# The four operand sums of an FFN chunk pair: made in the up stage from the tiles on chip and stored, instead of in the down stage

## The chip, the cores and the metric

The kernel runs on one core of one Trainium2 chip. The metric is the device time of one execution in microseconds (us); the median of three runs stands for the kernel. Engines: PE (TensorE matmul), DVE (VectorE), ACT (ScalarE), POOL (GpSimd), and SP (SyncE), which here only issues DMAs.

## The reference

One layer of a streaming encoder on 1024 tokens and 16 meta tokens, 1024 channels, in float32. The change lies in the last third, the convolutional FFN:

```python
def _conv_ffn(xn, w_up, conv_w, conv_b, w_down):
    hid = xn @ w_up                                   # 1024 -> 2 * 2816
    hp = jnp.pad(hid, ((0, 0), (CONV_WIDTH - 1, 0), (0, 0)))
    conv = conv_b + sum(hp[:, j:j + seq_len] * conv_w[j] for j in range(CONV_WIDTH))
    val, gate = jnp.split(conv, 2, axis=-1)
    return (jax.nn.silu(gate) * val) @ w_down         # 2816 -> 1024
```

Before it come an RMSNorm and a mixer (forgetting attention beside a state-space branch, merged and projected); behind it the residual sum, a final RMSNorm, and the meta tokens are dropped.

## The kernel before, in words

Every float32 matmul is made of three PE products of rounded parts: each operand is split into hi (a copy on ACT that rounds) and lo (operand minus hi, function `split_lo`, line 137, on DVE or POOL). One logical product so costs hi·hi, hi·lo and lo·hi.

**Up stage (about 790 to 1230 us of the span).** The 2816 hidden channels are worked off in 22 chunks of 128; chunk c needs a gate block and a value block of `w_up`. Chunks 0, 1, 2 and 21 are made plainly (`plain_pair`); chunks 3 to 20 by `block_pair`, in which `seven` (line 213) replaces the eight block products of a 2x2 blocked matmul by seven, with sums of the weight blocks (`weight_forms`, `combine`: tiles `sf`, POOL, line 1286), split by ACT (line 1160) and DVE (line 137) into a ring of 8 tiles `sw`, and with sums of the token blocks that are made once. The seven products are put together from PSUM (banks `mm`, `sp`, `tp`) with ACT copies and DVE adds (line 238) into `hg` and `hv` (128 x 1026, in a ring of three); `c1`, `u2` and `u3` are scratch of `seven`. `seven` is also called once in the mixer (the GLU). Then the convolution of width 3: one ACT instruction (line 1336) and two DVE instructions (line 1338) for each of `og` and `ov` (lines 1197 and 1199 in plain chunks). `glue` (line 1167) makes the chunk's result: silu on ACT (line 1168), the product of value and gate on POOL (line 1169), and a store of 512 KB by SP to `a_d` in DRAM (line 1170). `og` and `ov` have one buffer each. Raw weights (`raw`) are loaded by SP, three buffers. During the up stage, `down_weight_sums` also makes the sums of `w_down`'s blocks in DRAM (`t_d`) by accumulating DMAs on POOL's queue (line 1304) and copies on SP's.

**Down stage (about 1230 us to the end).** The product with `w_down` is also made by seven products over 2x2 blocks. Pair j holds chunks 2j and 2j+1; a11 and a21 are the left and right token halves (512 each) of chunk 2j, a12 and a22 those of chunk 2j+1. The 11 pairs are summed in four groups of pairs, [0-1], [2-4], [5-7], [8-10]; in each group the products run in the order 0, 4, 1, 2, 5, 3, 6. `load_pair` loads a pair's four halves (tiles `ar`, SP, line 1376) when the group's first product is prepared. `forms` (line 1380) prepares one product of one pair: it loads the weight (`wr`, SP, line 1383, a ring of 8), makes the operand's sum in place on POOL for products 1, 2, 3 and 6 (lines 1388, 1390, 1392, 1394), rounds operand and weight on ACT (line 1400), and splits off lo on POOL for products 0, 4 and 5, else on DVE. The results go to operand slots, 14 in all (`op`, and the former token tiles `xhi`, `xlo`). `product` (line 1437) issues the matmuls (lines 1455 to 1457: for a group of three pairs 36 of 512 columns, nine into each of four PSUM banks) and adds the PSUM banks into `u2`, `hs` on DVE (line 1465). `finish` makes the final norm.

The order of instructions on each engine is not that of the code: a scheduler, which simulates the program's times, decides it from the dependences. So a change of code can move instructions that it doesn't touch.

Of the kernel before, what the change touches and what calls it, by code (L numbers as in the profile page):

```python
# [9 lines left out]
F = mybir.dt.float32  # L10
# [4 lines left out]
ALU = mybir.AluOpType  # L15
# [43 lines left out]
def block_kernel(ctx, tc, x, meta, xbt, x0t, g1t, w_q, w_k, w_v, w_f, w_u, w_g, b_f, w_ao, lam_d, bw_d, cw_d,  # L59
# [56 lines left out]

    to_d = {p: dp.tile([D // 2, 512], F, name=f"to_d{p}") for p in (1, 2, 3, 5)}
    t_d = {p: dp.tile([DFF // 2, 512], F, name=f"t_d{p}") for p in (1, 2, 3, 5)}

    def stack(pl, t, n):  # L120
        s_ = pl.tile([P, KD, 64], R, tag="stk", name="stk")
# [91 lines left out]
    def seven(pl, A, B, kh, pieces, shift, top, bot):  # L213
# [4 lines left out]
        wide = max(n for _, n in pieces)  # L218
        st = []
        for p0, n in pieces:  # L220
            c1, u2, u3 = (pl.tile([P, wide], F, tag=tag, name=tag, bufs=2)[:, :n] for tag in ("c1", "u2", "u3"))
            st.append(dict(p0=p0, n=n, c1=c1, u2=u2, u3=u3, l=slice(p0, p0 + n),
                           r=slice(shift + p0, shift + p0 + n)))

        def prod(q, key, bank, a, b):
            joins = bank is None
# [15 lines left out]
        for q in st:  # L242
            add(q["u2"], prod(q, "b", s_ps, S2, T2), q["c1"])
        for q in st:
            S.copy(top[:, q["l"]], prod(q, "a", None, A12, B21))
        for q in st:
            add(q["u3"], prod(q, "b", None, S3, T3), q["c1"])
        for q in st:
# [918 lines left out]
    def glue(g_, v_, c):  # L1167
        S.activation(g_, g_, AF.Silu)  # L1168
        (V if c == NFF - 1 else GP).tensor_tensor(v_, v_, g_, ALU.mult)  # L1169
        (S if c == NFF - 1 else SY).dma_start(a_d[P * c:P * c + P], v_)  # L1170

    def conv_out(m, tag):
        if m % NFF == NFF - 1:

            return ha.tile([P, SEQ], F, tag="h", name=tag, bufs=3, padded_shape=[P, 2 * NH])
        return ha.tile([P, SEQ], F, tag=tag, name=tag)

    def plain_steps(c, parts=(QBLK,), ws={}):
        res = []
# [78 lines left out]
            SY.dma_start(h2[:, 4:], xc[:, 4:])  # L1258
    st_sm.close()
    ha = pool(st_r, "hid", side="right")  # L1260
    for tag in ("og", "ov"):
        ha.tile([P, SEQ], F, tag=tag, name=tag)
    normed(0, hm, 2)

    first_pair = plain_steps(0, ([(514, 256), (770, 254)], [(0, 258), (258, 256)]), early)
# [102 lines left out]
    def behind(ld, j):  # L1368
        if h_load and j in groups[1]:
            after(ld, h_load[-1])  # L1370

    def load_pair(j):
        for k in range(2):
            c0 = P * (2 * j + k)
            for h_ in range(2):
                behind(SY.dma_start(raw_tile(j, k, h_), a_d[c0:c0 + P, 512 * h_:512 * h_ + 512]), j)
# [1 line left out]
    n_op = [0]  # L1378

    def forms(p, j):  # L1380
        r = pairs[j]
        b_ = down1.tile([P, 512], F, tag="w", name="wr", bufs=8)
        behind(SY.dma_start(b_, w_block(*own_w[p], j) if p in own_w else t_d[p][P * j:P * j + P]), j)

        a11, a21, a12, a22 = (r[k, h_] for k in range(2) for h_ in range(2))
        sub, add = ALU.subtract, ALU.add
        if p == 1:
            GP.tensor_tensor(a11, a11, a21, sub)
        elif p == 2:
            GP.tensor_tensor(a11, a22, a11, add)  # L1390
        elif p == 3:
            GP.tensor_tensor(a21, a22, a21, sub)
        elif p == 6:
            GP.tensor_tensor(a11, a11, a12, sub)
        slot = ops[n_op[0] % len(ops)]
        n_op[0] += 1
        a_ = (a11, a11, a11, a21, a12, a22, a11)[p]
        eng = GP if p in (0, 4, 5) else V
        for q, src in ((0, a_), (2, b_)):
            hi = S.copy(slot[q], src)  # L1400
            if first_copy and j < 2 and p >= 5:
                after(hi, first_copy[1])
            cut = split_lo(eng, slot[q + 1], src, slot[q])
            if first_add and eng is V and j < 2 and p > 2:
                after(cut, first_add[1 if p == 3 else 3])
        return slot
# [88 lines left out]
    def prepare():  # L1495

        while len(ready) < (len(items) if first_add else 3) and room[0] >= len(groups[items[len(ready)][0]]):
            g, p = items[len(ready)]
            room[0] -= len(groups[g])
            if p == 0:  # L1500
                for j in groups[g]:
                    load_pair(j)
            ready[g, p] = [forms(p, j) for j in groups[g]]

    dpool[0] = down1
    for j in groups[0]:
        load_pair(j)
    for p in ORDER[:2]:
        room[0] -= 2
        ready[0, p] = [forms(p, j) for j in groups[0]]  # L1510
# [423 lines left out]
```

## Time and profile before

| | us |
|---|---|
| runs | 1465.48, 1460.87, 1460.35 |
| median | 1460.87 |
| profiled execution | 1462.22 |
| its span, first to last instruction | 1460.1 |
| mean granted PE clock | 0.994 |
| PE busy | 1429.3 |
| DVE / POOL / ACT busy | 1075.5 / 758.5 / 721.9 |

All details are from the one profiled execution. A row of the timeline gives the start in us, the duration, engine, source line, operation, output tile <- input tiles, shape, and in square brackets the idle time before it with the instruction that ended it. A row of the waits gives the waiting group, what ended its waits, their sum in us, their number, and the longest. A row of the groups gives line, engine, operation, tiles, shape and count, then busy time and mean ns of one, then idle time before and what ended it. A row of DMA issues gives tiles, queue, count, KB each and the median us from issue to landing. A row of stretches gives the busy time of each engine with its instructions, the granted PE clock (1 is full), the DMA engines' share and GB/s.

### The profile page before, as it was taken

What the parts mean: (1) busy time and instruction counts of PE and PEld (TensorE: products, weight loads), DVE (VectorE), ACT (ScalarE), POOL (GpSimd) and SP (SyncE); (2) the same over time, 40 slices, a digit from 0 to 9 for tenths busy, and PEclk for the clock granted to TensorE, in tenths of its full rate; (3) what the DMA queues carried; (4) which work ended last, traced back from release to release, by engine and by line L of the source; (5) the groups of instructions that cost most, each with busy time, mean ns of one, the idle gap of its engine ahead of it and who ended that gap; (6) DMA issues with size and microseconds to landing.
All of it is one profiled execution on the core that took longest, in us unless ns stands there. A gap on an engine that the chain in (4) does not pass through costs nothing. (4 is left out here: it accounts for less than half of the span.)

```text
span 1460.1 us, 26545 instructions
## 1 busy us (share of the span) xinstructions
PE 1429.3 (98%) x9646; PEld 1350.1 (92%) x9646; DVE 1075.5 (74%) x2200; ACT 721.9 (49%) x1421; POOL 758.5 (52%) x890
## 2 busy tenths in 40 slices
PE   8999999999999999999999999999999999998997
PEld 8999999988999999999889999999999999786886
DVE  7999788842757676656479977888887666788685
ACT  7646576422646565533646444444444435642433
POOL 1542147631556556425861235546544427889766
PEclk9999999999999999999999999999999999999998
DMA  7685644630137422167954246667753224866413
GB/s 288 171 188 161 150 111 115 161 116 30 37 124 164 128 65 69 41 234 249 251 149 145 73 109 177 177 174 176 172 138 109 87 83 150 302 196 179 132 36 115
DMA packets 89717, 209.31 MB, mean 143 GB/s; under 512 B 14498, under 2 KB 22322, under 8 KB 89204
## 3 DMA queue, kind: packets, MB, share of 16 engines
q1 hardware_dynamic: 70068, 162.55, 34.1%
q0 software_dynamic: 17792, 41.41, 14.8%
q10 hardware_dynamic: 1728, 3.68, 0.7%
q8 instruction: 76, 1.25, 0.4%
q14 instruction: 53, 0.43, 0.1%
HBM read 168.52 MB, written 69.35 MB: 163 GB/s over the span
## 5 line engine op out<-in xcount | busy, mean ns | idle before, releaser
L170 PE MATMUL mm<-xhi,whi 128*128 128x342 f32 (+2 forms) x480 | 156.9, 327 | 1.5 <-DVE q L137 1.0
L171 PE MATMUL mm<-xlo,whi 128*128 128x342 f32 (+2 forms) x480 | 155.6, 325 | 0.0
L172 PE MATMUL mm<-xhi,wlo 128*128 128x342 f32 (+2 forms) x480 | 155.4, 324 | 0.0
L1169 POOL TENSOR_TENSOR ov<-ov,og 128x1024 f32<-128x1024 f32 x21 | 51.1, 2434 | 124.5 <-ACT og L1168 120.6
L137 DVE TENSOR_TENSOR sw<-sf,sw 128x512 fp32r<-128x512 f32 x72 | 68.9, 957 | 51.7 <-ACT sw L1160 51.6
L1160 ACT CAST sw<-sf 128x512 fp32r<-128x512 f32 x72 | 44.9, 624 | 105.6 <-POOL sf L1286 71.7
L170 PEld LDWEIGHTS mm<-xhi,whi 128*128 128x128 f32 x480 | 90.6, 189 | 2.9 <-PE sp L804 0.8
L171 PEld LDWEIGHTS mm<-xlo,whi 128*128 128x128 f32 x480 | 90.6, 189 | 0.4 <-issue 0.2
L172 PEld LDWEIGHTS mm<-xhi,wlo 128*128 128x128 f32 x480 | 90.4, 189 | 0.3
L853 ACT CAST th<-tp 128x256 fp32r<-128x256 f32 (+3 forms) x120 | 56.1, 472 | 62.1 <-PE tp L846 29.4
L137 DVE TENSOR_TENSOR tl<-tp,th 128x256 fp32r<-128x256 f32 (+3 forms) x120 | 65.1, 547 | 25.1 <-ACT th L853 23.6
L1286 POOL TENSOR_TENSOR sf<-raw 128x512 f32<-128x512 f32 x36 | 47.5, 1319 | 68.4 <-ACT sw L1160 22.1
L1286 POOL TENSOR_TENSOR sf<-raw,sf 128x512 f32<-128x512 f32 x36 | 59.9, 1663 | 44.4 <-DVE sw L137 43.2
L234 PE MATMUL mm<-xhi,sw 128*128 128x258 f32 (+1 forms) x288 | 81.1, 282 | 0.0
L232 PE MATMUL mm<-xhi,sw 128*128 128x258 f32 (+1 forms) x288 | 80.9, 281 | 0.0
L233 PE MATMUL mm<-xlo,sw 128*128 128x258 f32 (+1 forms) x288 | 80.8, 281 | 0.0
L818 POOL TENSOR_SCALAR pt<-pt,nm 128x144 f32<-128x144 f32 (+4 forms) x72 | 52.2, 738 | 50.4 <-DVE nm L817 49.5
L1338 DVE SCALAR_TENSOR_TENSOR ov<-hv,cwt,ov 128x1024 f32<-128x1024 f32 x36 | 72.1, 2003 | 0.2
L1160 ACT CAST sw<-raw 128x512 fp32r<-128x512 f32 x70 | 43.0, 621 | 49.0 <-PE sp L234 22.3
L816 ACT ACTIVATE pt<-pt,nm 128x144 f32<-128x144 f32 (+4 forms) x72 | 52.9, 736 | 27.0 <-DVE nm L815 26.6
L809 DVE CUSTOM_DVE_ANT_0 pt<-sp,fb 128x328 f32<-128x328 f32 (+8 forms) x112 | 46.4, 430 | 19.5 <-PE sp L804 11.3
L137 DVE TENSOR_TENSOR sw<-raw,sw 128x512 fp32r<-128x512 f32 x70 | 55.0, 788 | 5.2 <-ACT sw L1160 4.7
(715 smaller groups left out, 5732.6 us busy)
## 6 DMA issues: line engine op xcount, KB each, us to landing
raw<-in_w_up_dram SPq DMA_DIRECT2D x44, 512.0 KB, 3.8
t_d<-in_w_dn_dram POOLq DMA_DIRECT2D x44, 256.0 KB, 6.7
ar<-a_d SPq DMA_DIRECT2D x44, 256.0 KB, 5.3
wr<-t_d SPq DMA_DIRECT2D x44, 256.0 KB, 2.8
a_d<-ov SPq DMA_DIRECT2D x21, 512.0 KB, 2.6
wr<-in_w_dn_dram SPq DMA_DIRECT2D x33, 256.0 KB, 4.2
t_d<-in_w_dn_dram SPq DMA_DIRECT2D x22, 256.0 KB, 4.2
t_d<-t_d SPq DMA_DIRECT2D x22, 256.0 KB, 4.7
```

The lines of the kernel that those rows point to most:

```text
L137: return eng.tensor_tensor(out_, src, hi.bitcast(F), ALU.subtract)
L170: yield PE.matmul(ps, whi[:, i, :], ahi[:, i], start=(i == 0), stop=False)
L171: yield PE.matmul(ps, whi[:, i, :], alo[:, i], start=False, stop=False)
L172: yield PE.matmul(ps, wlo[:, i, :], ahi[:, i], start=False, stop=(i == k - 1))
L232: PE.matmul(ps, a[0][:, i], bh, start=(i == 0 and not joins), stop=False, skip_group_check=True)
L233: PE.matmul(ps, a[0][:, i], bl, start=False, stop=False, skip_group_check=True)
L234: PE.matmul(ps, a[1][:, i], bh, start=False, stop=(i == kh - 1), skip_group_check=True)
L816: S.activation(pt[:n, :kc], pt[:n, :kc], AF.Exp, bias=nm[:n, 1:2], scale=0.125, accum_out=nm[:n, 2:3])
L853: S.copy(th[:kn, z:tw], tp[:kn, z:tw])
L1160: S.copy(hi, src)
L1286: sums.append(GP.tensor_tensor(f_, a, b, op))
L1338: V.scalar_tensor_tensor(out=o, in0=h_[:, j:SEQ + j], scalar=cwc(j, m), in1=o, op0=ALU.mult, op1=ALU.add)
```

## The change

The four sums of each of the pairs 0 to 9 are made in `glue`, at the end of the odd chunk, out of the even chunk's result (kept on chip: `ov` now has two buffers) and the odd chunk's. They are written over the two tiles of the even and odd chunk that have served (`e_` is the even chunk's `ov`, `g_` the odd chunk's `og`), and stored by SP to new DRAM arrays `s_d`. Of the even chunk only the left half is stored to `a_d`, since only a11 is loaded alone; of the odd chunk both. In the down stage `load_form` loads each form's operand by itself: seven loads of 256 KB a pair instead of four, and no sum. Pair 10 (chunks 20 and 21) stays as it was.

To make room on chip for the second `ov`, `seven` no longer has the scratch tiles `u2` and `u3`: their sums go into the right halves of the output tiles, which are overwritten later. For that, the copy of the product A12 is cut by two columns, so that it ends at the left half.

```diff
@@ -116,6 +116,7 @@
 
     to_d = {p: dp.tile([D // 2, 512], F, name=f"to_d{p}") for p in (1, 2, 3, 5)}
     t_d = {p: dp.tile([DFF // 2, 512], F, name=f"t_d{p}") for p in (1, 2, 3, 5)}
+    s_d = {p: dp.tile([DFF // 2, 512], F, name=f"s_d{p}") for p in (1, 2, 3, 6)}
 
     def stack(pl, t, n):
         s_ = pl.tile([P, KD, 64], R, tag="stk", name="stk")
@@ -218,9 +219,9 @@
         wide = max(n for _, n in pieces)
         st = []
         for p0, n in pieces:
-            c1, u2, u3 = (pl.tile([P, wide], F, tag=tag, name=tag, bufs=2)[:, :n] for tag in ("c1", "u2", "u3"))
-            st.append(dict(p0=p0, n=n, c1=c1, u2=u2, u3=u3, l=slice(p0, p0 + n),
-                           r=slice(shift + p0, shift + p0 + n)))
+            c1 = pl.tile([P, wide], F, tag="c1", name="c1", bufs=2)[:, :n]
+            right = slice(shift + p0, shift + p0 + n)
+            st.append(dict(p0=p0, n=n, c1=c1, u2=top[:, right], u3=bot[:, right], l=slice(p0, p0 + n), r=right))
 
         def prod(q, key, bank, a, b):
             joins = bank is None
@@ -242,7 +243,8 @@
         for q in st:
             add(q["u2"], prod(q, "b", s_ps, S2, T2), q["c1"])
         for q in st:
-            S.copy(top[:, q["l"]], prod(q, "a", None, A12, B21))
+            n = min(q["n"], shift - q["p0"])
+            S.copy(top[:, q["p0"]:q["p0"] + n], prod(q, "a", None, A12, B21)[:, :n])
         for q in st:
             add(q["u3"], prod(q, "b", None, S3, T3), q["c1"])
         for q in st:
@@ -1167,13 +1169,30 @@
     def glue(g_, v_, c):
         S.activation(g_, g_, AF.Silu)
         (V if c == NFF - 1 else GP).tensor_tensor(v_, v_, g_, ALU.mult)
-        (S if c == NFF - 1 else SY).dma_start(a_d[P * c:P * c + P], v_)
+        l_, r_ = HALF
+        rows = a_d[P * c:P * c + P]
+        if c % 2 == 0 and c < NFF - 2:
+            SY.dma_start(rows[:, l_], v_[:, l_])
+            even[0] = v_
+            return
+        (S if c == NFF - 1 else SY).dma_start(rows, v_)
+        if c >= NFF - 2:
+            return
+        e_, j = even[0], c // 2
+        GP.tensor_tensor(e_[:, l_], e_[:, l_], e_[:, r_], ALU.subtract)
+        GP.tensor_tensor(g_[:, l_], v_[:, r_], e_[:, l_], ALU.add)
+        GP.tensor_tensor(e_[:, r_], v_[:, r_], e_[:, r_], ALU.subtract)
+        GP.tensor_tensor(g_[:, r_], g_[:, l_], v_[:, l_], ALU.subtract)
+        for p, t_ in ((1, e_[:, l_]), (2, g_[:, l_]), (3, e_[:, r_]), (6, g_[:, r_])):
+            SY.dma_start(s_d[p][P * j:P * j + P], t_)
+
+    even = [None]
 
     def conv_out(m, tag):
         if m % NFF == NFF - 1:
 
             return ha.tile([P, SEQ], F, tag="h", name=tag, bufs=3, padded_shape=[P, 2 * NH])
-        return ha.tile([P, SEQ], F, tag=tag, name=tag)
+        return ha.tile([P, SEQ], F, tag=tag, name=tag, bufs=OUTS[tag])
 
     def plain_steps(c, parts=(QBLK,), ws={}):
         res = []
@@ -1258,8 +1277,9 @@
             SY.dma_start(h2[:, 4:], xc[:, 4:])
     st_sm.close()
     ha = pool(st_r, "hid", side="right")
-    for tag in ("og", "ov"):
-        ha.tile([P, SEQ], F, tag=tag, name=tag)
+    OUTS = {"og": 1, "ov": 2}
+    for tag, n in OUTS.items():
+        ha.tile([P, SEQ], F, tag=tag, name=tag, bufs=n)
     normed(0, hm, 2)
 
     first_pair = plain_steps(0, ([(514, 256), (770, 254)], [(0, 258), (258, 256)]), early)
@@ -1369,6 +1389,21 @@
         if h_load and j in groups[1]:
             after(ld, h_load[-1])
 
+    LAST = NFF // 2 - 1
+    FROM = {0: (0, 0), 4: (1, 0), 5: (1, 1)}
+
+    def load_form(p, j):
+        t_ = dpool[j % 4 // 2].tile([P, 512], F, tag={0: "a00", 4: "a01", 1: "a10", 2: "a11", 5: "a00", 3: "a01", 6: "a10"}[p],
+                                    name="ar", bufs=2)
+        if p in FROM:
+            k, h_ = FROM[p]
+            c0 = P * (2 * j + k)
+            src = a_d[c0:c0 + P, 512 * h_:512 * h_ + 512]
+        else:
+            src = s_d[p][P * j:P * j + P]
+        behind(SY.dma_start(t_, src), j)
+        return t_
+
     def load_pair(j):
         for k in range(2):
             c0 = P * (2 * j + k)
@@ -1378,23 +1413,26 @@
     n_op = [0]
 
     def forms(p, j):
-        r = pairs[j]
         b_ = down1.tile([P, 512], F, tag="w", name="wr", bufs=8)
         behind(SY.dma_start(b_, w_block(*own_w[p], j) if p in own_w else t_d[p][P * j:P * j + P]), j)
 
-        a11, a21, a12, a22 = (r[k, h_] for k in range(2) for h_ in range(2))
-        sub, add = ALU.subtract, ALU.add
-        if p == 1:
-            GP.tensor_tensor(a11, a11, a21, sub)
-        elif p == 2:
-            GP.tensor_tensor(a11, a22, a11, add)
-        elif p == 3:
-            GP.tensor_tensor(a21, a22, a21, sub)
-        elif p == 6:
-            GP.tensor_tensor(a11, a11, a12, sub)
+        if j == LAST:
+            r = pairs[j]
+            a11, a21, a12, a22 = (r[k, h_] for k in range(2) for h_ in range(2))
+            sub, add = ALU.subtract, ALU.add
+            if p == 1:
+                GP.tensor_tensor(a11, a11, a21, sub)
+            elif p == 2:
+                GP.tensor_tensor(a11, a22, a11, add)
+            elif p == 3:
+                GP.tensor_tensor(a21, a22, a21, sub)
+            elif p == 6:
+                GP.tensor_tensor(a11, a11, a12, sub)
+            a_ = (a11, a11, a11, a21, a12, a22, a11)[p]
+        else:
+            a_ = load_form(p, j)
         slot = ops[n_op[0] % len(ops)]
         n_op[0] += 1
-        a_ = (a11, a11, a11, a21, a12, a22, a11)[p]
         eng = GP if p in (0, 4, 5) else V
         for q, src in ((0, a_), (2, b_)):
             hi = S.copy(slot[q], src)
@@ -1499,12 +1537,11 @@
             room[0] -= len(groups[g])
             if p == 0:
                 for j in groups[g]:
-                    load_pair(j)
+                    if j == LAST:
+                        load_pair(j)
             ready[g, p] = [forms(p, j) for j in groups[g]]
 
     dpool[0] = down1
-    for j in groups[0]:
-        load_pair(j)
     for p in ORDER[:2]:
         room[0] -= 2
         ready[0, p] = [forms(p, j) for j in groups[0]]
```

In numbers: SP's loads of `ar` go from 44 to 74, its stores to `a_d` stay 21 (ten of them of half the size), and 40 stores of 256 KB to `s_d` come in. PE, DVE and ACT have as many instructions as before; POOL too, 40 of its sums having changed place.

The rows below are each engine's instructions in their order in the program: line, operation, output tile <- input tiles, shape.

On POOL in the up stage, at the end of an even chunk and of the odd chunk after it (1169 or 1171 is the product of value and gate, 1286 or 1306 a weight sum, 1304 or 1324 an accumulating DMA). Before:

```order
L1169 TENSOR_TENSOR ov<-ov,og 128x1024
L1286 TENSOR_TENSOR sf<-raw,sf 128x512
L1286 TENSOR_TENSOR sf<-raw 128x512 x2
L1304 DMA t_d_89<-in_w_dn_dram 128x512
L1304 DMA t_d_87<-in_w_dn_dram 128x512
L1304 DMA t_d_88<-in_w_dn_dram 128x512
L1304 DMA t_d_90<-in_w_dn_dram 128x512
L1286 TENSOR_TENSOR sf<-raw,sf 128x512
L1169 TENSOR_TENSOR ov<-ov,og 128x1024
L1286 TENSOR_TENSOR sf<-raw,sf 128x512
L1286 TENSOR_TENSOR sf<-raw 128x512 x2
```

Now, at an odd chunk's product:

```order
L1306 TENSOR_TENSOR sf<-raw,sf 128x512
L1171 TENSOR_TENSOR ov<-ov,og 128x1024
L1183 TENSOR_TENSOR og<-ov 128x512
L1184 TENSOR_TENSOR ov<-ov 128x512
L1306 TENSOR_TENSOR sf<-raw,sf 128x512
L1185 TENSOR_TENSOR og<-og,ov 128x512
L1306 TENSOR_TENSOR sf<-raw 128x512 x2
L1324 DMA t_d_89<-in_w_dn_dram 128x512
L1324 DMA t_d_87<-in_w_dn_dram 128x512
L1324 DMA t_d_88<-in_w_dn_dram 128x512
L1324 DMA t_d_90<-in_w_dn_dram 128x512
```

Two of the four sums (1183, 1184) stand between the odd chunk's product and the next weight sum, and a third (1185) behind that sum. The first one (1182) needs the even chunk alone and stands earlier, between two weight sums.

On DVE at the change from one chunk to the next (238 or 239 is an add of `seven` out of PSUM, 1338 or 1358 a convolution step, 137 or 138 a split of a weight). Before:

```order
L1338 SCALAR_TENSOR_TENSOR ov<-hv,cwt,ov 128x1024
L238 TENSOR_TENSOR hg<-tp,u_11926 128x256
L1338 SCALAR_TENSOR_TENSOR ov<-hv,cwt,ov 128x1024
L137 TENSOR_TENSOR sw<-raw,sw 128x512
L1338 SCALAR_TENSOR_TENSOR og<-hg,cwt,og 128x1024
L137 TENSOR_TENSOR sw<-sf,sw 128x512
L1338 SCALAR_TENSOR_TENSOR og<-hg,cwt,og 128x1024
L238 TENSOR_TENSOR u_12171<-sp,c_12170 128x258
L238 TENSOR_TENSOR u_12174<-sp,c_12173 128x256
```

Now, at the same chunk:

```order
L1358 SCALAR_TENSOR_TENSOR ov<-hv,cwt,ov 128x1024
L239 TENSOR_TENSOR hg<-tp,hg 128x256
L138 TENSOR_TENSOR sw<-raw,sw 128x512
L1358 SCALAR_TENSOR_TENSOR ov<-hv,cwt,ov 128x1024
L1358 SCALAR_TENSOR_TENSOR og<-hg,cwt,og 128x1024
L239 TENSOR_TENSOR hg<-sp,c_12150 128x258
L1358 SCALAR_TENSOR_TENSOR og<-hg,cwt,og 128x1024
L239 TENSOR_TENSOR hg<-sp,c_12151 128x256
L138 TENSOR_TENSOR sw<-sf,sw 128x512
```

The first of the two adds out of `sp` (into `u`, now into `hg`) stood behind both convolution steps of `og`, and now stands between them; the split of a weight sum that was ahead of it is now behind. In other chunks the two orders differ less.

On POOL at the start of the down stage (137 or 138 with `op`, `xhi` or `xlo` is a split for an operand slot; 1388 to 1394 are the sums). Before:

```order
L137 TENSOR_TENSOR op_15256<-ar,op_15256 128x512
L1388 TENSOR_TENSOR ar<-ar 128x512
L1392 TENSOR_TENSOR ar<-ar 128x512
L137 TENSOR_TENSOR op_15257<-ar,op_15257 128x512
L137 TENSOR_TENSOR xhi<-ar,xhi 128x512
L137 TENSOR_TENSOR op_15259<-ar,op_15259 128x512
L1388 TENSOR_TENSOR ar<-ar 128x512
L137 TENSOR_TENSOR xhi<-ar,xhi 128x512
L1390 TENSOR_TENSOR ar<-ar 128x512
L137 TENSOR_TENSOR op_15256<-wr,op_15256 128x512
```

Now:

```order
L138 TENSOR_TENSOR op_15239<-wr,op_15239 128x512
L138 TENSOR_TENSOR op_15239<-ar,op_15239 128x512
L1171 TENSOR_TENSOR ov<-ov,og 128x1024
L138 TENSOR_TENSOR xlo<-ar,xlo 128x512
L138 TENSOR_TENSOR xlo<-wr,xlo 128x512
L138 TENSOR_TENSOR xlo<-ar,xlo 128x512
L138 TENSOR_TENSOR xlo<-wr,xlo 128x512
L138 TENSOR_TENSOR op_15236<-wr,op_15236 128x512
```

The sums are gone from between the splits, which now follow each other; the product of chunk 20 (1171) stands among them.

## The prediction

> **What bounds the kernel now.** I read the page's totals first, then stretches of 40 us, then PE's waits in the last stretch, then the chain behind each.
>
> ```profile
> PE 1429.3 (98%) x9646; PEld 1350.1 (92%) x9646; DVE 1075.5 (74%) x2200; ACT 721.9 (49%) x1421; POOL 758.5 (52%) x890
> ```
>
> PE is busy in 1429.3 of 1460.1 us, so 31 us is about all that anything other than less PE work can win, and this change leaves PE's work as it is. What counts is where PE stands still.
>
> ```profile
> core 0: us, PE busy (x) PEld busy (x) DVE busy (x) ACT busy (x) POOL busy (x), PEclk, DMA share, GB/s
> 800.00:840.00 40.00, 38.36 (x245) 38.19 (x244) 39.97 (x58) 19.24 (x32) 12.29 (x6) 1.00 0.24 80
> 920.00:960.00 40.00, 40.00 (x338) 40.00 (x338) 33.24 (x44) 17.33 (x28) 22.02 (x19) 1.00 0.71 187
> 1240.00:1280.00 40.00, 37.95 (x166) 30.67 (x165) 30.62 (x36) 26.07 (x49) 34.60 (x23) 1.00 0.81 293
> 1280.00:1320.00 40.00, 40.00 (x176) 32.61 (x174) 34.83 (x38) 15.12 (x29) 36.26 (x25) 1.00 0.57 184
> 1320.00:1360.00 40.00, 35.68 (x147) 28.54 (x147) 34.53 (x41) 14.93 (x28) 29.81 (x23) 0.96 0.74 210
> 1360.00:1400.00 40.00, 40.00 (x177) 33.05 (x176) 27.26 (x32) 15.27 (x30) 37.05 (x27) 1.00 0.30 86
> ```
>
> The up stage proper (the row from 920 stands for it) has PE full, POOL half free (22.0 of 40) and DVE with 6.8 us to spare in 40. Where it starts (800 to 840) DVE has nothing to spare, and PE loses 1.6. In the down stage (from about 1230) POOL is near full and PE loses time twice. Its waits from 1180 on:
>
> ```profile
> PE mm L1455 <- ACT xlo L1400: 3.0, 1, 3.0
> PE tp L1455 <- DVE hs L1465: 2.6, 2, 1.9
> PE mm L1455 <- DVE hs L1465: 1.1, 1, 1.1
> PE sp L1457 <- POOL op L137: 1.0, 1, 1.0
> PE sp L1455 <- DVE hs L1465: 0.6, 1, 0.6
> ```
>
> The 1.9 in the second row is the last product's (at 1448) and the 1.1 is the first fill (at 1244); neither has to do with the sums. The others come from operands that are late. The longest and the 1.0, in PE's order of time:
>
> ```profile
> 1275.80 0.39 PE L1457 MATMUL tp<-op 128*128 128x512 f32 x1
> 1277.15 0.50 PE L1457 MATMUL sp<-op 128*128 128x512 f32 x1 [0.96 <-POOL op L137]
> 1277.48 0.40 PE L1457 MATMUL tp<-op 128*128 128x512 f32 x1
> ...
> 1337.47 0.39 PE L1456 MATMUL po<-xlo 128*128 128x512 f32 x1
> 1337.69 0.39 PE L1457 MATMUL po<-xlo 128*128 128x512 f32 x1
> ...
> 1341.11 0.47 PE L1455 MATMUL mm<-xlo 128*128 128x512 f32 x1 [3.03 <-ACT xlo L1400]
> ...
> 1343.03 0.63 PE L1457 MATMUL mm<-xlo 128*128 128x512 f32 x1
> 1343.45 0.63 PE L1455 MATMUL mm<-op 128*128 128x512 f32 x1
> ...
> 1345.07 0.39 PE L1456 MATMUL mm<-xlo 128*128 128x512 f32 x1
> ```
>
> Normal spacing is 0.22 to 0.23 us (1337.47 to 1337.69). After the long wait it is 0.42 until 1345.07, with the granted clock at 0.96 over that stretch. So this one wait costs 3.42 − 0.23 = 3.2, and then ten steps that take 3.96 instead of 2.3: 4.9 in all. The one at 1275.8 costs 1.68 − 2 × 0.23 = 1.2. The Trainium skill, "TensorE: Matmul & The Clock Gate", section "Part 1: The HAM clock gate", says that an idle window of about 3.4 us halves PE's clock until it has been busy about as long. The trace agrees in kind: 3.2 us of idling was enough here and 1.35 was not, so a long wait costs half as much again as itself.
>
> Why ACT was late at 1341:
>
> ```profile
> 1335.23 0.62 ACT L1400 CAST xhi<-ar 128x512 fp32r<-128x512 f32 x1 [4.73 <-POOL ar L1390]
> ```
>
> ACT's queue stood 4.7 us behind one of POOL's sums (line 1390), and the cast that PE needed was in the queue behind it.
>
> **What goes from the down stage.** 40 of the 44 sums leave POOL there:
>
> ```profile
> L1394 POOL TENSOR_TENSOR ar<-ar 128x512 f32<-128x512 f32 x11 | 17.9, 1669 | 6.9 <-DVE xlo L137 4.4 <-DVE xhi L137 2.5
> L1390 POOL TENSOR_TENSOR ar<-ar 128x512 f32<-128x512 f32 x11 | 17.8, 1621 | 2.3 <-DVE xhi L137 2.3
> L1392 POOL TENSOR_TENSOR ar<-ar 128x512 f32<-128x512 f32 x11 | 17.4, 1580 | 0.1
> L1388 POOL TENSOR_TENSOR ar<-ar 128x512 f32<-128x512 f32 x11 | 17.3, 1570 | 0.2
> ```
>
> 70.4 us × 40/44 = 64 us of POOL, out of some 138 that it is busy from 1240 to 1400. ACT then waits for a load instead of for POOL. I count as won: 4.9 (1337), 1.2 (1275), and the waits of 0.6 and 0.7 (2.6 − 1.9) for DVE's adds with 0.27 of restart each (what the one at 1275 cost beyond its 0.96), since DVE's splits are slowed by POOL's sums (below): 1.8. Together **−8.0**. What is late next: the first fill and the last product stay as they are.
>
> **What comes into the down stage.** Seven operands a pair are loaded instead of four: 30 loads more of 256 KB, 7.9 MB. Over the 200 us that is 39 GB/s on a mean of 193 in the four rows above, whose largest is 293; and each load is now issued when its form is due, no longer four at a pair's start.
>
> ```profile
> ar<-a_d SPq DMA_DIRECT2D x44, 256.0 KB, 5.3
> ...
> a_d<-ov SPq DMA_DIRECT2D x21, 512.0 KB, 2.6
> ...
> 1249.57 0.62 ACT L1400 CAST op<-ar 128x512 fp32r<-128x512 f32 x1 [2.19 <-DMA ar<-a_d]
> ```
>
> A form's weight goes through a ring of 8, its operand through pairs of buffers that come round after three products or more. A product of three pairs has 36 matmuls, 8.2 us at 0.227; a load may so run 8/3 × 8.2 = 22 us ahead, against 5.3 to land. That hides it in the steady part. At the start (1240 to 1280, DMA share 0.81) ACT already waits 2.2 for a load. Bounds 0 to +4.9 (one more wait like that of 1337). I take **+1.0**, near the lower, since that wait of ACT held no matmul up.
>
> **What comes into the up stage.** Four sums a pair on POOL, 1.29 us each where nothing disturbs (the `sf` rows here, of the same shape), and the stores:
>
> ```profile
> 936.67 2.40 POOL L1169 TENSOR_TENSOR ov<-ov,og 128x1024 f32<-128x1024 f32 x1 [5.86 <-ACT og L1168]
> ...
> 939.76 1.29 POOL L1286 TENSOR_TENSOR sf<-raw,sf 128x512 f32<-128x512 f32 x1 [0.69 <-DVE sw L137]
> 941.13 1.28 POOL L1286 TENSOR_TENSOR sf<-raw 128x512 f32<-128x512 f32 x1
> ...
> 949.58 1.25 ACT L1336 ACTIVATE og<-hg,cwt 128x1024 f32<-128x1024 f32 x1 [1.54 <-DVE hg L238]
> ```
>
> POOL has room: 22.0 + 4 × 1.29 to 1.75 is under 29 of 40. In an odd chunk three sums stand between line 1169's product and the `sf` of line 1286, and make the latter 2.6 to 3.9 us late; the weights made of them are used some 12 us later, so nothing is felt. Behind POOL, SP's queue holds the four stores and then the next `raw`, which is a chunk ahead. `og` has one buffer: the last sum ends about 939.1 + 4 × 1.3 = 944.3, its store lands 2.6 later, and ACT writes `og` again at 949.6, so 2.7 us are left.
>
> What is felt is DVE, when POOL runs beside it:
>
> ```profile
> 819.51 0.68 DVE L271 TENSOR_TENSOR fb<-fa 128x514 f32<-128x514 f32 x1
> ...
> 833.66 1.74 POOL L1286 TENSOR_TENSOR sf<-raw 128x512 f32<-128x512 f32 x1
> ...
> 834.17 1.78 DVE L271 TENSOR_TENSOR fb<-fa 128x514 f32<-128x514 f32 x1
> ```
>
> The same operation takes 1.78 instead of 0.68: a sum costs DVE 1.1 us where DVE reads two operands from SBUF. The Trainium skill, "SBUF — State Buffer", section "Who interferes with whom", says that such a DVE instruction and a GpSimd one that reads SBUF exclude each other for a whole instruction. That speaks against this change: by it a sum would cost DVE up to its own 1.29, 5.2 a pair for the 4.4 below.
>
> Pair 0 (chunks 0 and 1) meets DVE in its full stretch: 4 × 1.1 = 4.4 us later, bounds 0 and 4.4. PE has other products to put in there, and did lose 1.6 of the 40, so I take half: **+2.2**. In the nine other pairs 4.4 in 40 fits DVE's 6.8, but at one place there is little slack:
>
> ```profile
> 935.42 0.74 DVE L238 TENSOR_TENSOR u<-sp,c 128x258 f32<-128x258 f32 x2
> ...
> 936.10 0.28 PE L232 MATMUL sp<-t2h,sw 128*128 128x258 f32 x1
> ...
> 934.22 1.27 DVE L1338 SCALAR_TENSOR_TENSOR og<-hg,cwt,og 128x1024 f32<-128x1024 f32 x1
> ```
>
> PE's product into `sp` follows the first of the two adds (935.8) by 0.3 us. A sum's 1.1 ahead of that add would cost 0.8 a pair, 7.2 in nine: bounds 0 to 7.2. In the changed order that add stands one conv earlier (1.27) in every second chunk, more than 1.1; so I am near the lower end: **+1.4**.
>
> The products' scratch (`u2`, `u3`), which goes into the output tiles, costs nothing: the same adds of the same size, and the tiles they write were free a chunk before.
>
> **Sum.** −8.0 + 1.0 + 2.2 + 1.4 = −3.4 us. The profiled execution took 1462.2 (span 1460.1 and 2.1 around it), 1.35 over the median of the three runs; carried to the median, 1460.9 − 3.4 = **1457.5**.
>
> **Rivals.**
> (a) The up stage pays nothing and the loads are hidden: −8.0, 1452.9. For it: POOL's 18 us free in 40. Against it: DVE's 39.97 of 40. 15%.
> (b) Slower: DVE. If POOL's sums fall on DVE in both chunks of a pair and the earlier place of the add doesn't help, both adds are late by 0.8: 9 × 1.6 + 4.4 = 18.8, less 8.0: +10.8, 1471.7. It decides from the point at which DVE is over 0.3 us late at the add, and half of it is enough to end above 1460.9. For it: 33.2 + 4.4 leaves 2.4 of 40. Against it: of a pair's four sums one falls where DVE waits for ACT. 15%.
> (c) Slower: the loads. If a load comes late once in each of the three later groups, each costs 4.9: +14.7 − 8.0 + 3.6 = +10.3, 1471.2. It needs landings of over 22 us. 8%.
> (d) It doesn't do what it says: PE's waits in the down stage remain, as ACT's order and DVE's adds set them, and only the 1.2 that was POOL's own goes: −1.2 + 3.6 = +2.4, 1463.3. 10%.
> My forecast has 52%.
>
> About 0.5% (7.3 us) is what a measurement of this kernel can tell from no change. Below 1453.6 lies (a), 15%; above 1468.2 lie (b) and (c), 23%; the rest is 62%. The range goes from 1452.5 to 1467: (a) and the forecast with its bounds (up to 1457.5 + 2.2 + 5.8, its up stage at the worst, about 1465.5), (d), and the milder half of (b).
>
> **What would show it.** Right: no PE wait over 1 us between 1250 and 1440 in the new trace, no slow matmuls in the down stage, POOL there at some 55% of the time; up stage rows with DVE at 36 to 38 of 40 and PE at 40. Wrong: PE waits on DVE's L239 adds in every pair (b), ACT's casts waiting on `ar<-s_d` for longer than they do now (c), or a gap of over 3 us with the clock below 0.98 again (d). More than two PE waits over 2 us in the up stage would make the forecast wrong whatever the down stage wins.

## The result, and the profile after

The changed kernel takes 1471.83 us (median of 4 runs, 1470.16 to 1474.03) against 1460.65 (4 runs, 1460.35 to 1465.48). The ratio is 1.0073, 95% interval 1.0055 to 1.0091: slower by 11 us, where 1457.5 was forecast, and outside the range. The profiled execution took 1472.26, its span is 1470.4, 10.3 more than before.

PE's waits from 790 on, in the changed kernel (what waits, what ended it: us in all, times, the longest):

```profile
PE sp L233 <- DVE hg L239: 4.9, 6, 0.9
PE mm L233 <- ACT c L242: 2.7, 2, 2.4
PE sp L234 <- DVE t1l L138: 2.2, 1, 2.2
PE tp L1493 <- DVE hs L1503: 2.1, 1, 2.1
PE mm L1212 <- DVE og L1218: 2.0, 1, 2.0
PE sp L233 <- ACT sw L1162: 0.5, 1, 0.5
```

All waits of the down stage are gone but that of its last product (line 1493). What is new lies in the up stage: six waits of nearly 1 us on the add of the second product (line 239), and three long ones (2.43, 2.21 and 1.99; the last was 1.6 before). The stretches say the same (PE, PEld, DVE, ACT, POOL busy, PE clock, DMA share, GB/s):

```profile
800.00:840.00 40.00, 37.54 (x231) 37.08 (x231) 39.90 (x56) 17.00 (x27) 15.77 (x9) 0.96 0.22 77
920.00:960.00 40.00, 38.21 (x305) 38.00 (x306) 31.32 (x42) 16.96 (x28) 25.59 (x21) 0.96 0.68 181
1240.00:1280.00 40.00, 40.00 (x197) 34.84 (x197) 25.70 (x37) 28.59 (x53) 21.21 (x15) 1.00 0.80 291
1320.00:1360.00 40.00, 40.00 (x177) 32.93 (x176) 24.18 (x36) 15.56 (x30) 21.29 (x18) 1.00 0.81 226
```

In the down stage PE is full and POOL at 21 of 40 instead of 30 to 36. In the up stage PE does 305 matmuls in the 40 us from 920 where it did 338.

To add this up I took, from the trace, each matmul's start to the next one's start, less 0.4625 ns a column (the unhindered spacing, 0.12 us for 258 columns; a remainder below nothing counts as nothing). What is left over, by stage, in us:

| | 0 to 790 | 790 to 860 | 860 to 1240 | 1240 to end | sum |
|---|---|---|---|---|---|
| before | 69.1 | 2.3 | 3.5 | 12.2 | 87.1 |
| changed | 70.1 | 7.4 | 17.4 | 2.5 | 97.4 |
| difference | +1.0 | +5.1 | +13.9 | −9.7 | +10.3 |

This is the whole difference of the spans. (In the first column, where the kernels do the same, twelve other traces lie between 65.2 and 69.3: so much differs from one execution to the next.) So there are three things: the down stage won 9.7, the stage's start lost 5.1, and the rest of the up stage 13.9.

**How the 13.9 come about.** POOL, ACT, DVE and PE around the boundary of chunks 8 and 9 in the changed kernel:

```profile
971.11 1.63 POOL L1183 TENSOR_TENSOR og<-ov 128x512 f32<-128x512 f32 x1
972.69 1.30 POOL L1184 TENSOR_TENSOR ov<-ov 128x512 f32<-128x512 f32 x1
973.95 1.29 POOL L1306 TENSOR_TENSOR sf<-raw,sf 128x512 f32<-128x512 f32 x1
975.20 1.28 POOL L1185 TENSOR_TENSOR og<-og,ov 128x512 f32<-128x512 f32 x1
976.43 1.30 POOL L1306 TENSOR_TENSOR sf<-raw 128x512 f32<-128x512 f32 x1
...
980.81 3.34 POOL L1324 DMA_DIRECT2D t_d<-in_w_dn_dram  x4
982.95 2.98 POOL L1306 TENSOR_TENSOR sf<-raw,sf 128x512 f32<-128x512 f32 x1
...
977.76 0.62 ACT L1162 CAST sw<-sf 128x512 fp32r<-128x512 f32 x1 [8.15 <-POOL sf L1306]
...
982.87 1.92 DVE L138 TENSOR_TENSOR sw<-raw,sw 128x512 fp32r<-128x512 f32 x1
984.72 2.30 DVE L1358 SCALAR_TENSOR_TENSOR ov<-hv,cwt,ov 128x1024 f32<-128x1024 f32 x1
...
988.14 0.41 DVE L239 TENSOR_TENSOR hg<-sp,c 128x258 f32<-128x258 f32 x1
...
988.61 0.39 PE L233 MATMUL sp<-t2h,sw 128*128 128x258 f32 x1 [0.88 <-DVE hg L239]
```

Two pair sums (1183, 1184) stand ahead of the first weight sum and a third (1185) ahead of the second, and ACT's queue waits 8.15 us for that second one. The chunk's last weight sum ends at 985.93, beside DVE's last split (0.68 undisturbed, here 1.92) and `ov`'s second convolution step (1.27, here 2.30). The add behind them comes 0.9 after PE is ready for it. The pair sums themselves lie beside little of DVE's work. The same place before:

```profile
966.22 3.32 POOL L1304 DMA_DIRECT2D t_d<-in_w_dn_dram  x4
968.36 2.51 POOL L1286 TENSOR_TENSOR sf<-raw,sf 128x512 f32<-128x512 f32 x1
...
962.30 0.62 ACT L1160 CAST sw<-sf 128x512 fp32r<-128x512 f32 x1 [4.79 <-POOL sf L1286]
...
969.60 2.35 DVE L1338 SCALAR_TENSOR_TENSOR ov<-hv,cwt,ov 128x1024 f32<-128x1024 f32 x1
971.88 0.68 DVE L137 TENSOR_TENSOR sw<-raw,sw 128x512 fp32r<-128x512 f32 x1
...
975.47 0.74 DVE L238 TENSOR_TENSOR u<-sp,c 128x258 f32<-128x258 f32 x2
```

There the last weight sum ended at 970.87, 5.2 before PE's next product into `sp` (976.06); now it ends 1.8 before the time at which PE would be ready (988.61 − 0.88 = 987.73).

What differs isn't how much POOL slows DVE. At this boundary DVE's splits and convolution steps take 3.0 us more than undisturbed in both kernels (1.60, 2.27 and 2.35 before; 1.45, 1.92 and 2.30 now). It is how late they run: ACT's cast in the rows starts 13.8 us ahead of PE's product before, and 10.0 us ahead of the time at which PE is ready now; `ov`'s second step 6.5 and 3.0.

The largest single loss, some 4.2 of the 13.9, comes the same way three chunks earlier:

```profile
915.73 4.04 DVE L1358 SCALAR_TENSOR_TENSOR ov<-hv,cwt,ov 128x1024 f32<-128x1024 f32 x1
...
916.48 2.20 POOL L1306 TENSOR_TENSOR sf<-raw,sf 128x512 f32<-128x512 f32 x1
...
920.20 1.24 ACT L1356 ACTIVATE og<-hg,cwt 128x1024 f32<-128x1024 f32 x1 [4.31 <-DVE hg L239]
```

This step took 4.05 us in the kernel before too (at 906.46), and no matmul waited: it started 0.7 us ahead of PE's product into `mm` (907.18), and now starts 2.3 us behind it (913.46). So the copy by ACT that PE needs next is late, PE waits 2.43 us, and the matmuls behind the wait run slowly for a while (last section).

**How the 5.1 come about.** Pair 0's sums beside a DVE that has no time to spare:

```profile
837.69 1.73 POOL L1183 TENSOR_TENSOR og<-ov 128x512 f32<-128x512 f32 x1
839.39 1.74 POOL L1184 TENSOR_TENSOR ov<-ov 128x512 f32<-128x512 f32 x1
841.10 1.74 POOL L1185 TENSOR_TENSOR og<-og,ov 128x512 f32<-128x512 f32 x1
...
839.90 1.78 DVE L138 TENSOR_TENSOR t2l<-fb,t2h 128x514 fp32r<-128x514 f32 x1
841.61 1.78 DVE L1337 TENSOR_TENSOR fb<-xhi,xlo 128x514 f32<-128x514 f32 x1
...
847.54 0.39 PE L234 MATMUL sp<-t1l,sw 128*128 128x258 f32 x1 [2.21 <-DVE t1l L138]
```

Here each sum costs DVE its 1.1 us, and about half of the 5.1 is the wait for the token form `t1l` that is then late. The other half lies at 816 to 823: pair 0's first sum (line 1182, at 813) had delayed DVE there as well, PE waits 0.5 for ACT and 1.99 instead of 1.6 for `og`, and the matmuls behind run slowly, at some 1.5 us (the clock of 0.96 in the row from 800). PE's order had changed too: products of chunk 3 stand ahead of chunk 2's last tiles. That isn't the cause: e5 below has the same order there and loses nothing.

### The profile page after: what moved, and what is told of

Its sections match the earlier page's. It is cut to its first block, busy times and chain, and to the rows that moved or that the text cites. A ratio compares the mean times of both kernels' runs of the same rounds, so it can differ in the third digit from the quotient of the medians.

```text
span 1470.4 us, 26722 instructions
## 1 busy us (share of the span) xinstructions
PE 1432.9 (97%) x9646; PEld 1351.8 (92%) x9646; DVE 1067.1 (73%) x2200; ACT 718.7 (49%) x1421; POOL 759.9 (52%) x890
## 5 line engine op out<-in xcount | busy, mean ns | idle before, releaser
L138 DVE TENSOR_TENSOR sw<-sf,sw 128x512 fp32r<-128x512 f32 x72 | 84.1, 1169 | 42.0 <-ACT sw L1162 42.0
L1306 POOL TENSOR_TENSOR sf<-raw,sf 128x512 f32<-128x512 f32 x36 | 63.5, 1763 | 39.6 <-DVE sw L138 39.5
L1306 POOL TENSOR_TENSOR sf<-raw 128x512 f32<-128x512 f32 x36 | 51.9, 1441 | 44.8 <-DMA raw<-in_w_up_dram 24.4
L138 DVE TENSOR_TENSOR sw<-raw,sw 128x512 fp32r<-128x512 f32 x70 | 67.5, 968 | 4.7 <-ACT sw L1162 4.6
L1358 DVE SCALAR_TENSOR_TENSOR ov<-hv,cwt,ov 128x1024 f32<-128x1024 f32 x36 | 63.4, 1761 | 0.5 <-ACT ov L1356 0.4
L848 PE MATMUL tp<-ident,pt 128*128 128x128 f32 (+1 forms) x360 | 58.4, 270 | 0.1
```

What stands on the lines that cost most here:

```text
L138: return eng.tensor_tensor(out_, src, hi.bitcast(F), ALU.subtract)
L848: PE.transpose(tp[:kn, o:o + n], p_[:n, k0:k0 + kn], ident[:n, :n])
L1306: sums.append(GP.tensor_tensor(f_, a, b, op))
L1358: V.scalar_tensor_tensor(out=o, in0=h_[:, j:SEQ + j], scalar=cwc(j, m), in1=o, op0=ALU.mult, op1=ALU.add)
```

## The experiments

Theories: **Q**, the sums' place in POOL's queue, ahead of the weight sums; **P**, the slowing of DVE by each sum wherever it stands; **S**, `seven`'s scratch; **L**, the stores. Each result is the median, and the ratio to the kernel before on the same chip with its interval. "Up" is the column 860 to 1240 of the table above, "start" 790 to 860, "down" 1240 to the end.

### Which part of the change it is

In e1 the four lines of `GP.tensor_tensor` in `glue` are left out, so the down stage multiplies what stands in the tiles instead of the sums.

> The changed kernel without its 40 sums on POOL in the up stage: s_d gets whatever stands in the tiles (so the down stage's operands are not the sums); stores, loads and seven's scratch stay. Theory Q (the sums stand in POOL's queue ahead of the weight sums sf, so ACT's and DVE's queues wait, and the convolutions are late): the up stage's PE waits go, 1452 to 1455. Theory P (each sum slows DVE by 1.1 us over the shared access to SBUF): the same, 1452 to 1455. Theory S (seven's scratch in the output tiles makes its adds wait): the waits on DVE hg stay, about 1469. Theory L (the stores hold up SP's queue and so the raw weights): they stay too, about 1470.

1451.68, ratio 0.9938 (0.9921 to 0.9954). Start 2.3, up 4.3, down 4.9. Without the sums nothing is lost, though all stores, loads and the scratch change are in: S and L fall, and the sums cost some 20 us (0.9938 against 1.0073).

e2 is the kernel before with `seven` of the changed kernel.

```diff
-            c1, u2, u3 = (pl.tile([P, wide], F, tag=tag, name=tag, bufs=2)[:, :n] for tag in ("c1", "u2", "u3"))
+            c1 = pl.tile([P, wide], F, tag="c1", name="c1", bufs=2)[:, :n]
+            right = slice(shift + p0, shift + p0 + n)
...
-            S.copy(top[:, q["l"]], prod(q, "a", None, A12, B21))
+            n = min(q["n"], shift - q["p0"])
+            S.copy(top[:, q["p0"]:q["p0"] + n], prod(q, "a", None, A12, B21)[:, :n])
```

> The kernel before with only seven's scratch change (u2 and u3 in the output tiles, the shorter copy). Theory S: PE waits on DVE's adds into hg in chunks 8 to 13, some 8 us, so about 1469. Theories Q, P and L: as before, 1460 to 1462.

1459.56, ratio 0.9985 (0.9971 to 0.9999). Start 2.3, up 3.9, down 11.7, as before. S falls a second time.

### The start of the stage

e4 leaves pair 0's sums in the down stage.

```diff
-        if c % 2 == 0 and c < NFF - 2:
+        if c % 2 == 0 and c // 2 in MADE:
...
-        if c >= NFF - 2:
+        if c // 2 not in MADE:
...
+    MADE = range(1, 10)
...
-        if j == LAST:
+        if j not in MADE:
...
```

> The changed kernel with pair 0's sums left in the down stage, as the last pair's are. The loss from 800 to 850 was 5.1 us more than in the kernel before. If it comes from pair 0's sums beside a DVE that has no time to spare, it goes: 1466 to 1468, with the up stage's later waits and a free down stage as they were; if pair 0's sums are then late at the start of the down stage, 1.4 of that comes back. If the loss there comes from something else (seven's scratch, the stores), 1471.

1465.45, ratio 1.0031 (1.0015 to 1.0047). Start 2.3 as before, up 17.5, down 5.1. The start's loss is pair 0's and nothing else's; against the changed kernel it is worth 6 us (1.0031 to 1.0073; each of the two is known to some 2.4 us). The sum of the up stage behind it is unchanged, so its loss doesn't come from the late start. Its make-up differs: eight waits on the add (6.2 us) instead of six, and 1.4 us instead of 2.43 at the wait on ACT.

### Place or pace

e3 leaves out the accumulating DMAs on POOL.

```diff
-            if 0 <= j < NFF // 2:
+            if 0 <= j < NFF // 2 and not more:
```

> The changed kernel without the 44 accumulating DMAs that POOL issues for w_down's sums (the sums of w_down's blocks are then incomplete). Each chunk's train on POOL is 3.3 us shorter. Theory Q: the waits of about 1 us in each of chunks 8 to 13 go, 8 us, and the wait at chunk 6 with them or not: 1459 to 1464. Theory P: the sums slow DVE as before, the waits stay, 1469 to 1472. Theory L: the stores stay, 1469 to 1472.

1460.7, ratio 0.9998 (0.9988 to 1.0009). Start 7.4 as in the changed kernel, up 5.1 instead of 17.4, down 2.4. With all 40 sums in place the up stage's waits are gone. Against P: what counts is the train of work on POOL, or the DMAs' traffic, which this run drops too (e9 keeps it).

e5 has fills in the place of the sums.

```diff
-        GP.tensor_tensor(e_[:, l_], e_[:, l_], e_[:, r_], ALU.subtract)
-        GP.tensor_tensor(g_[:, l_], v_[:, r_], e_[:, l_], ALU.add)
-        GP.tensor_tensor(e_[:, r_], v_[:, r_], e_[:, r_], ALU.subtract)
-        GP.tensor_tensor(g_[:, r_], g_[:, l_], v_[:, l_], ALU.subtract)
+        GP.memset(e_[:, l_].bitcast(BF), 0.0)
+        a_ = GP.memset(g_[:, l_].bitcast(BF), 0.0)
+        b_ = GP.memset(e_[:, r_].bitcast(BF), 0.0)
+        after(b_, a_)
+        after(GP.memset(g_[:, r_].bitcast(BF), 0.0), b_)
```

> The changed kernel with each of the 40 sums on POOL replaced by a fill of the same tile half (1024 elements of two bytes, which read nothing; a fill of 128x1024 takes 0.96 us on POOL, a sum 1.3 to 1.7), three of them between the odd chunk's product and the next weight sum; s_d then holds zeros, the down stage's operands are not the sums. If a fill leaves DVE's pace alone (to be read from DVE's rows beside it): theory Q (POOL's queue is what costs): the waits of about 1 us on DVE hg in chunks 8 to 13 stay, 1465 to 1471; theory P (the slowing of DVE by sums): they go, 1452 to 1456.

One of the four groups of fills on POOL (busy us, mean ns, idle before):

```profile
L1183 POOL MEMSET og<- 128x1024 bf16 x10 | 9.5, 951 | 0.5
```

A split of DVE at the start, beside the fills of pair 0 (832.94 to 835.67):

```profile
834.25 0.69 DVE L138 TENSOR_TENSOR t2l<-fb,t2h 128x514 fp32r<-128x514 f32 x1
```

PE's waits on the add (us in all, times, the longest):

```profile
PE sp L233 <- DVE hg L239: 5.2, 10, 1.2
```

1459.3, ratio 0.9995 (0.9981 to 1.001): outside both ranges that were expected. Start 2.3, up 12.3, down 2.4. The fills leave DVE's pace alone: its split takes 0.69 us, where beside a sum it took 1.78. The waits on the add are there all the same (10 of them, 5.2), with nothing but fills of 0.95 us in the sums' places on POOL: Q, for 8.8 of the 13.9 of the up stage. The start costs nothing here, where the sums cost 5.1, though PE's order there is that of the changed kernel (chunk 3's products ahead of chunk 2's last tiles, at 839 to 843): so it is the slowing of DVE by the sums that costs there, P, and not PE's order. These 5.1 are about what the time is below the range for Q.

e6 makes the sums of pairs 1 to 9 on DVE (`GP.tensor_tensor` becomes `V.tensor_tensor`; `MADE` as in e4).

> Pairs 1 to 9 summed in the up stage as changed, but on DVE (0.68 us each where nothing disturbs) instead of POOL; pair 0 summed in the down stage. Theory Q: POOL's queue is that of before, DVE has 6.8 us to spare in 40 and gets 2.7; the steady waits go, the transition at 800 is that of before: 1451 to 1455. Rival (DVE's own order: the sums stand ahead of the convolutions, and whatever is put on DVE makes the adds late): waits of about 1 us in every odd chunk, 1460 to 1465.

1461.16, ratio 1.0004 (0.9988 to 1.002). Start 2.3, up 13.0, down 2.4. The rival of this run was right in time and place: on DVE the sums stand ahead of the convolutions, which then fall beside POOL's weight sums. (The single waits are smaller than it said: five of 0.5 at most and three of up to 1.1 on DVE's adds.) At one place:

```profile
962.39 1.77 DVE L1184 TENSOR_TENSOR ov<-ov 128x512 f32<-128x512 f32 x1
...
973.47 2.91 DVE L138 TENSOR_TENSOR sw<-raw,sw 128x512 fp32r<-128x512 f32 x1
976.30 2.30 DVE L1359 SCALAR_TENSOR_TENSOR og<-hg,cwt,og 128x1024 f32<-128x1024 f32 x1
...
974.54 2.97 POOL L1307 TENSOR_TENSOR sf<-raw,sf 128x512 f32<-128x512 f32 x1
```

So it isn't only POOL's queue: what makes the convolutions late on DVE's own queue costs too, here 9.5 us for nine pairs.

### Only the order

e9 is e4 with one dependence moved, so that POOL's four DMA issues stand behind the weight sum that came after them (the last one ahead of the next product of value and gate). No instruction is added or dropped. The order on the other engines isn't quite the same, since the scheduler answers: at these boundaries DVE splits the weight sum ahead of the first add out of `sp` instead of behind both, ACT makes one copy ahead of the silu, a matmul changes its place, and SP's loads do. On DVE this puts the add 0.6 us later, so DVE's order doesn't explain a gain.

```diff
-        down_weight_sums(c - 3, sums[n_])
+        down_weight_sums(c - 3, sums[n_ + 1])
```

> The kernel of e4_without_pair0 (sums of pairs 1 to 9 on POOL in the up stage) with one dependence moved: the accumulating DMAs that POOL issues for w_down's sums come behind the second weight sum of their chunk instead of behind the first. All else stands in the same order. Theory Q: that weight sum comes 3.3 us earlier, the casts, splits and convolutions behind it follow, and the waits of about 1 us in chunks 7 to 13 go: 1465.4 less 8 to 12, 1453 to 1457. Theory P (DVE is slowed by the sums wherever they are): 1463 to 1466. If POOL's DMA issues hurt the convolutions beside which they now stand: about 1460.

1452.94, ratio 0.9954 (0.9937 to 0.9972): against e4's 1.0031 it wins 11 us, and it is faster than both kernels. Start 2.3, up 4.1, down 5.2. The same boundary:

```profile
965.99 2.17 POOL L1307 TENSOR_TENSOR sf<-raw,sf 128x512 f32<-128x512 f32 x1
968.10 3.33 POOL L1325 DMA_DIRECT2D t_d<-in_w_dn_dram  x4
...
961.88 0.62 ACT L1162 CAST sw<-sf 128x512 fp32r<-128x512 f32 x1 [7.84 <-POOL sf L1307]
...
968.63 1.27 DVE L1359 SCALAR_TENSOR_TENSOR ov<-hv,cwt,ov 128x1024 f32<-128x1024 f32 x1
...
971.62 0.41 DVE L239 TENSOR_TENSOR hg<-sp,c 128x258 f32<-128x258 f32 x1
...
972.92 0.28 PE L233 MATMUL sp<-t2h,sw 128*128 128x258 f32 x1
```

The last weight sum takes 2.17 instead of 2.98 and ends at 968.16, 4.8 before PE's product; the convolution step at 968.63 runs beside DMA issues and takes its 1.27. The add ends at 972.03, 0.9 before PE needs it. ACT still waits 7.84 us for a weight sum; DVE's splits and steps are slowed by 1.8 us here, instead of 3.0.

e12 makes the same move in the changed kernel itself, pair 0 included.

> The changed kernel itself, pair 0 included, with only that one dependence moved (the accumulating DMAs behind the second weight sum of their chunk). If the two causes are apart, POOL's queue (from chunk 6 on) and pair 0 beside the full DVE (800 to 850), only the second stays: 1471.8 less 10 to 13, 1459 to 1462, with 5 us lost from 800 to 850 and no wait of about 1 us behind it. If they feed each other (the chunks run late because the transition did), 1453 to 1456 or, the other way, 1466 and more.

PE's waits from 790 on, without three that are as in the changed kernel:

```profile
PE sp L234 <- DVE t1l L138: 2.2, 1, 2.2
...
PE sp L233 <- DVE hg L239: 0.3, 1, 0.3
```

1457.45, ratio 0.9988 (0.9973 to 1.0003). Start 8.8, up 5.4, down 2.6. The time is 1.6 below the range for two causes apart and 1.5 above the one for causes that feed each other; the columns decide it: the start's loss is all there (with 1.5 us of slow matmuls more than in the changed kernel), the up stage's is gone. The two causes are apart: the move wins 12 us (0.9988 against 1.0073), and what stays against e9 (0.9954) is pair 0's 5.

### Sums for the later pairs only

e7 and e8 set `MADE = range(7, 10)` and `range(5, 10)` in e4; e10 is e8 with the dependence of e9 moved; e11 is e7 with this line:

```diff
-        eng = GP if p in (0, 4, 5) else V
+        eng = GP if p in (0, 4, 5) and not (p == 0 and j in groups[2]) else V
```

> Pairs 5 to 9 (chunks 10 to 19) are summed in the up stage, on POOL. Theory Q: chunks 10 to 13 lose about 1 us each as in the changed kernel (4 to 5), and the down stage's wait of 4.9 at 1337 goes: 1459 to 1462. Theory P: the same and 4 more, 1463 to 1466.

1455.19, ratio 0.9973 (0.9958 to 0.9987), below both of the ranges that were expected. Up 7.1, down 4.9. The wait at 1337 is gone, as expected, and chunks 10 to 13 lose less than expected (2.4 us more than before in 950 to 1090).

> The kernel of e8_from5 (sums of pairs 5 to 9 in the up stage) with the same dependence moved. Theory Q: of the 3.5 us that its up stage loses against the kernel before, 2.5 to 3.5 come back: 1452 to 1453. Otherwise 1455.

1452.99, ratio 0.9955 (0.994 to 0.997). Up 3.4, down 5.6: the move gives the up stage back in full here too. It isn't told apart from e9.

> Only pairs 7 to 9 (chunks 14 to 19) are summed in the up stage, on POOL; pairs 0 to 6 in the down stage as before. In chunks 14 to 19 POOL issues two accumulating DMAs a chunk or fewer. Theory Q: no PE wait over 0.4 in these chunks, the up stage within 1.5 us of before; in the down stage the waits of before at 1275 (1.2) and on DVE (1.8) stay, the one at 1337 (4.9) goes if it comes from the sums of pairs 7 and later and stays if from 5 and 6: 1456 or 1461. Theory P: the sums cost 1.1 each wherever they are: three pairs lose some 4 us in the up stage, 1460 or 1465.

1466.51, ratio 1.0043 (1.0027 to 1.0058), over both of the times that were expected. Up 4.0: in the up stage the three pairs cost nothing, as Q had it. Down 17.2, by a wait that no theory had:

```profile
1327.81 3.88 POOL L1430 TENSOR_TENSOR ar<-ar 128x512 f32<-128x512 f32 x2
1330.84 2.09 POOL L138 TENSOR_TENSOR xhi<-ar,xhi 128x512 fp32r<-128x512 f32 x1
...
1337.01 2.02 POOL L138 TENSOR_TENSOR xhi<-wr,xhi 128x512 fp32r<-128x512 f32 x1
...
1328.39 11.20 DVE L138 TENSOR_TENSOR op<-wr,op 128x512 fp32r<-128x512 f32 x1
...
1343.92 0.77 PE L1493 MATMUL mm<-xlo 128*128 128x512 f32 x1 [9.56 <-DVE u L1503]
```

One split of DVE, 0.68 us of work, stands 11.2 us, from POOL's two sums to the end of its six splits, and the adds that PE waits for stand behind it.

> The kernel of e7_from7 with the six splits of the third group's first product on DVE instead of POOL. There DVE stood 11.2 us in one split of 0.68 while POOL ran two sums and six splits without a pause, and PE waited 9.6. If it is POOL's unbroken run that kept DVE out, the run is now four sums long at most and the wait shrinks to 3 or less: 1457 to 1460. If the wait comes from the loads or from ACT's order (the mixed group of pairs with and without sums), it stays: 1465 to 1467.

1461.39, ratio 1.0011 (0.9998 to 1.0024). The 9.6 is gone, and DVE's longest instruction there is 3.0; PE waits 2.6 once instead (down 8.4). So it was POOL's splits at this place that kept DVE out. That they ran without a pause isn't enough by itself (last section). The median is above what was expected by 1.4.

## Why the prediction was wrong, point by point

- **The down stage (−8.0, and +1.0 for the loads): right, and a little short.** It won 9.7. (The terms of −8.0 add up to 7.9.) No PE wait is left between 1250 and 1440, the first fill's wait of 1.1, which was to stay, went too, and the seven loads a pair cost nothing.
- **Pair 0 (+2.2, bounds 0 to 4.4): mechanism right, size off, above the upper bound too.** It measured 5.1 in the profile and 5 to 6 by the ratios of e12 against e9 and of the changed kernel against e4. I took half because PE "has other products to put in there". It had none that it could run: its next products waited for what DVE had late, `og` and the token form `t1l`, and the slow matmuls behind one of these waits (some 1.5 us) were in no term.
- **The nine other pairs (+1.4, bounds 0 to 7.2): this is the step that failed.** It measured 13.9. The prediction saw that three sums make the weight sums "2.6 to 3.9 us late" and went on: "the weights made of them are used some 12 us later, so nothing is felt". The weights were indeed not late. But behind a weight sum's cast and split, in ACT's and DVE's queues, stand the convolution and the one add with 0.3 us of slack, and they came some 3 us later against PE. The price that the prediction did put on this place, a pair sum's 1.1 ahead of the add, wasn't what was paid: POOL slows DVE there no more than before. I looked only at whom the pair sums themselves would meet. e9, which moves four DMA issues behind a weight sum, takes the up column from e4's 17.5 to 4.1, 11 us by the ratios.
- **Rival (b), slower by DVE, 1471.7, at 15%**, has the time nearly to the digit, by luck, and the place (the add into `sp`, 0.9 late at the worst). Its mechanism, the pair sums beside DVE, is only that of the start; in the up stage it would have cost all nine pairs alike, where chunks 14 to 20 lost almost nothing. There POOL issues two DMAs a chunk or fewer.
- **Rivals (a), (c) and (d)** are out: ACT's longest wait for a load from 1240 on is 1.3, where it was 2.3, and the down stage does what was said.
- **The signs.** Those of the down stage came (POOL at 21 of 40, 53%). Those of the up stage did not: from 920 PE has 38.2 of 40, and DVE 31.3, not 36 to 38 and no more than the 33.2 of before. The sign of (b), waits on the adds of line 239, came in six chunks and not in every pair.
- **What I argued from room** ("POOL has room", 22.0 of 40; "4.4 in 40 fits DVE's 6.8") was true and told nothing. e9's DVE and POOL do the same work as e4's, and PE is full.

What stays open: how much of the add's delay comes through ACT's queue (8.15 us behind a weight sum, ahead of `ov`'s first convolution step), and how much through the last weight sum beside DVE's last split and step. In e9 ACT's wait is still there (7.84) and its cast 11.0 us ahead of PE's product, and the add is in time; so at that boundary ACT's wait alone isn't enough. No run gives the two shares, and the chunks may feed each other's delay. e9, like e4, loses 4.0 at its last product where the changed kernel loses 2.1; the cause is open.

## What to carry to other kernels

When an instruction goes into an in-order queue, follow what it pushes back, not only what it does: the pushed ones meet other work on other engines, and a place with 0.3 us of slack may be there. Room in a stretch of 40 us says nothing on that; the order of rows within one period does. A slowing that costs nothing in the kernel before, as the 4.05 us for a step of 1.27, costs once the work comes 3 us later. And before a change is given up for such a loss, look for work in the same queue that nobody waits for soon, here the DMA issues, and put that behind: one dependence turned a loss of 5 us (e4) into a gain of 7 (e9).

## What the runs showed of the hardware

- Beside POOL's two-operand instructions a DVE instruction with two operands from SBUF may not get in for long: 11.20 us for 0.68 of work (e7). The Trainium skill, "SBUF — State Buffer", section "Who interferes with whom", has the one that comes first hold the shared ports for its whole instruction; here DVE was kept out over eight POOL instructions. A run of POOL without a pause isn't enough for that: in e11 POOL made six splits from 1312.85 to 1322.15 without one, and three splits of DVE beside them (from 1315.87 on) took 1.75 to 1.77 us each, by turns; in the changed kernel DVE got in by turns with pair 0's sums, too. What decides between the two isn't shown. In e7 POOL's six splits start 1.2 us apart, in e11's run up to 1.7. So a sum's 1.1 us is the price where the two take turns, and no upper bound.
- The clock of PE fell after shorter waits than the 3.2 us of before. In the changed kernel it is 0.83 from 918 to 928, around a wait of 2.43, with matmuls of 258 columns spaced 0.21 instead of 0.12:

```profile
921.76 0.56 PE L233 MATMUL mm<-xhi,sw 128*128 128x258 f32 x1 [2.43 <-ACT c L242]
...
922.33 0.42 PE L235 MATMUL mm<-xhi,sw 128*128 128x258 f32 x1
922.55 0.42 PE L233 MATMUL mm<-xhi,sw 128*128 128x258 f32 x1
```

The wait of 2.21 at 847 left the clock at 1.00. In e12 the same wait (2.2, at 846) did not: 0.79 from 844 to 852. So the length of one wait doesn't decide it.
